# An FFN up-projection in three token blocks of 768 instead of two of 1152

## The chip, the core and the metric

The kernel runs on one NeuronCore of a Trainium2 chip. The metric is device time in microseconds (us) of one launch. Engines are named as the profile names them: PE (TensorE, matmuls) and PEld (its weight loads), DVE (VectorE), ACT (ScalarE), POOL (GpSimd), SP (SyncE, which here only issues DMAs).

## The reference

One encoder layer over 2048 + 256 tokens (2304 in all, two groups with the same weights), float32. The change lies in its second half, the convolutional FFN:

```
x = x + jnp.concatenate([m_out, a_out], axis=-1) @ w_out
h = rmsnorm(x, norm2_w)
u = centred_dwconv(h @ w_up, conv_w, conv_b)      # width 3 over tokens, 2*2816 columns
a, g = jnp.split(u, 2, axis=-1)
return x + (jax.nn.silu(g) * a) @ w_down          # then a last rmsnorm
```

D_MODEL is 1024, D_FF is 2816 = 22 column blocks of 128, so `w_up` has 44 column blocks, 22 for the gate g and 22 for a.

## The kernel before

Four stretches follow each other: a projection with preparation of q and k, mLSTM and attention interleaved, the output projection (`phase_c`), then the **up-pass** (`phase_u`) and the **down-pass** (`phase_e`). Tokens lie along the free dimension, channels on the 128 partitions.

**Products.** Every float32 operand is split in two float32r parts, hi (a rounded copy, made by ACT) and lo (the rest, a subtraction on DVE), and a product takes three matmuls: hi·hi, hi·lo, lo·hi. On top of that both passes use a 2x2 block scheme with seven products in place of eight (Strassen's, in Winograd's order), which needs sums of weight blocks and sums of token blocks.

**The up-pass.** The tokens are taken in blocks of `BLK`; `DT` holds the borders of the columns that a block computes (one or more columns beyond the block, for the width-3 convolution, which `carry` hands to the next block). For each block, 11 **groups** (`for gi, gr in enumerate(groups)`) each make two calls of `up`: one for two column blocks of the gate, one for the two of a. A call (`up_start` and its `rest`) loads two column blocks of `w_up` (`ru`, two DMAs of 512 KB on SP's queue), makes three sums `tw` and one in place on POOL, and runs seven products `mul` named "11", "21", "t2", "t1", "t3", "22", "t4". Each `mul` splits a 128x512 weight block into a `wu` (ACT copy, DVE subtraction; five rotating buffers, `WU`) and multiplies it with the operand of that name in `ops`, which holds a half of the block's tokens (n columns), hi and lo. The results come out of PSUM tiles p1, p2, p3 (`pa`, `pb`, `pc` in the profile) into `u` by ACT copies and DVE additions; p1 is accumulated on further after each copy. `conv` then makes `y` on ACT and two DVE multiply-adds per column block; in the last block ACT mends the two columns where the token groups meet. A group ends with two DVE products y·silu(g), four POOL sums for the down-pass's block scheme, and seven POOL-issued stores into DRAM `a_d`.

**Operands of the up-pass.** `n2_d` in DRAM holds the normed tokens; `n2_sums` makes their block sums on POOL (through DRAM `n2t_d`) and `n2_load` brings each of the seven operands in two halves (SP DMA, ACT copy, DVE subtraction). The sums for block b+1 are made in groups 3 to 6 (`SG`) of block b. The first three operands (`EARLY`) lie in the pool `d_1`, the others in `d_l` and `d_r`; all have one buffer, so those of block 1 are loaded when block 0 has done with them.

**The down-pass.** Seven products over 11 pairs of channel blocks and `G3` = 3 stretches of 384 token columns (z), with rings of weights (`dw` staged, `we` split) and of token operands (`te`, split in the same way). It is written behind the up-pass, in SBUF that the up-pass gives back.

**Order.** Each engine works through its own instructions in order. A list scheduler with a time model sorts the program's instructions into these queues at build time, so that products of the next call stand between those of the current one; `high_priority` pulls marked code ahead.

Of the kernel before, what the change touches and what calls it, by code (L numbers as in the profile page):

```python
# [35 lines left out]
BLK = 1152  # L36
# [10 lines left out]
NH = 580  # L47
NW = 2 * NH + 1
DT = (0, 2 * NH, T)
HB = BLK // 2  # L50
TW = T // 2
N2A, N2B = 1280, 1024
# [33 lines left out]
P0 = ((V, V),) * 4  # L86
P1 = ((V, V),) * 7
LOP = ()
DLAG = 6
SEGS = ((0, NT1), (NT1, NT))  # L90
# [944 lines left out]
def phase_c(g, sn, sp, pp, wps):  # L1035
# [64 lines left out]
    def tail_b(b, x, ps, r):  # L1100
        r = rstd_rows(g, ps, r, BT)
        for z in range(NCC):
            nc.vector.scalar_tensor_tensor(x[:, z], x[:, z], g.n2w[:, z:z + 1], r, ALU.mult, ALU.mult)
            if z % 4 == 3:
                if b * BT < N2A:
                    g.st.dma_start(g.n2_d[0][:, z - 3:z + 1, b * BT:(b + 1) * BT], x[:, z - 3:z + 1])
                if b * BT >= N2B:
                    g.st.dma_start(g.n2_d[1][:, z - 3:z + 1, b * BT - N2B:(b + 1) * BT - N2B], x[:, z - 3:z + 1])
        g.normed.add(b)
# [10 lines left out]
    for n, b in enumerate(order):  # L1120
        x, mx = nxt
        for z in range(4):
# [14 lines left out]
            if (n, z) > (5, 0) and sums:  # L1137

                n2_sums(g, sp, 0, sums.pop(0), tag="rn", bufs=2)
# [9 lines left out]
EARLY, LATE = OPS[:3], OPS[3:]  # L1149
# [7 lines left out]
def n2_load(g, ops, b, k, engs=("vector", "vector")):  # L1157
# [4 lines left out]
    if k[0] == "t":  # L1162
        i, h = SUMS[k]
        src = g.n2t_d[b, i, :, :, h]
    else:
        t = DT[b] - (0, N2B)[b] + n * (int(k[1]) - 1)
        src = g.n2_d[b][:, NCC // 2 * (int(k[0]) - 1):, t:t + n]
    for z in range(0, NCC // 2, 2):
# [3 lines left out]
        getattr(nc, engs[z // 2]).tensor_tensor(lo, f32(lo), f32(hi), ALU.subtract)  # L1172
# [6 lines left out]
def n2_sums(g, pool, b, c, engs=("gpsimd",) * 4, tag="tc", bufs=3):  # L1179
# [4 lines left out]
    m = n // 2  # L1184
    for z in range(2):
        rs = []
        for k in range(2):
            r = pool.tile([P, NH], F32, tag=tag, name=f"rn{b}_{c}_{z}_{k}", bufs=bufs)[:, 0:n]
            r = r.rearrange("p (h t) -> p h t", h=2)
            src = g.n2_d[b][:, c + NCC // 2 * k, DT[b] - (0, N2B)[b]:DT[b + 1] - (0, N2B)[b]].rearrange("p (h t) -> p h t", h=2)  # L1190
            nc.gpsimd.dma_start(r, src[:, :, z * m:z * m + m])
            rs.append(r)
        (b11, b12), (b21, b22) = ((r[:, 0], r[:, 1]) for r in rs)
        for eng, (o, p, q) in zip(engs, ((b11, b12, b11), (b12, b22, b12), (b22, b22, b11), (b21, b21, b22))):
            getattr(nc, eng).tensor_tensor(o, p, q, ALU.subtract)
        for k in range(2):
            nc.gpsimd.dma_start(g.n2t_d[b, k, :, c, :, z * m:z * m + m], rs[k])
# [17 lines left out]

def up_start(g, s1, bank, ops, b, jj, rs=None):
# [4 lines left out]
    m = n // 2  # L1221
# [6 lines left out]
    def mul(p, k, src, add=False):  # L1228
# [6 lines left out]
        for z in range(2):  # L1235
            for c in range(NCC // 2):
                for i, (aa, bb) in enumerate(((0, 0), (0, 1), (1, 0))):
                    nc.tensor.matmul(p[:, z], w[:, aa, c, :], ops[k][:, c, bb, z * m:z * m + m],  # L1238
                                     start=c == 0 and i == 0 and not add, stop=c == NCC // 2 - 1 and i == 2,
                                     skip_group_check=add)  # L1240
    p1, p2 = bank("a" + nm)[:, :, 0:m], bank("b" + nm)[:, :, 0:m]
# [8 lines left out]
    def rest(u1, u2):  # L1250


        u11, u12, u21, u22 = (u[:, k * n:k * n + n].rearrange("p (z t) -> p z t", z=2) for u in (u1, u2) for k in range(2))
# [10 lines left out]
        p3 = bank("c" + nm)[:, :, 0:m]  # L1264
# [14 lines left out]
def phase_u(g, tc, s1, pd, ops, first):  # L1279
# [5 lines left out]
    with ExitStack() as st:  # L1285
        sa = st.enter_context(tc.tile_pool(name="d_a", bufs=1, reuse_waits="tile"))
        for k in range(YB):
            sa.tile([P, BLK], F32, tag="y", name=f"place_y{k}", bufs=YB)
        for k in range(3):
            sa.tile([P, NH], F32, tag="tc", name=f"place_tc{k}", bufs=3)  # L1290
# [18 lines left out]
        late.update(n2_ops(sl2, 0, ("t3", "t1")))  # L1309
        late = {k: late[k] for k in LATE}  # L1310
        for k, e in zip(LATE, P0):
            n2_load(g, late, 0, k, engs=e)
# [3 lines left out]
        def bank(nm):  # L1316
            return banks(g, pd[(g.nbank + 1) // 2 % 2], "p" + nm)
        for b in range(ND):
            nn = DT[b + 1] - DT[b]
            if b:  # L1320
                ops = n2_ops(s1[0], b, EARLY)
                ops.update(n2_ops(sl, b, ("t4", "22")))
                ops.update(n2_ops(sl2, b, ("t3", "t1")))
                for k, e in zip(OPS, P1):
                    n2_load(g, ops, b, k, engs=e)
# [33 lines left out]
            for gi, gr in enumerate(groups):  # L1359
                if b < ND - 1 and SG <= gi < SG + NCC // 2:  # L1360
                    n2_sums(g, sa, b + 1, gi - SG)
                ygs = up(gr[0] + NFC)
# [6 lines left out]
                t1, t2, t4 = (sa.tile([P, NH], F32, tag="tc", name=f"tc{k}_{b}_{gi}", bufs=3)[:, 0:HB] for k in (1, 2, 4))  # L1369
# [11 lines left out]
def phase_e(g, tc, pd):  # L1381
# [5 lines left out]
    with ExitStack() as st:  # L1387
        sx = st.enter_context(tc.tile_pool(name="e_t", bufs=1, reuse_waits="tile"))
        for k in range(TR):
            sx.tile([P, 2, TG, CG], F32R, tag="t", name=f"place_t{k}", bufs=TR)  # L1390
        swa = st.enter_context(tc.tile_pool(name="e_w", bufs=1, reuse_waits="tile"))
        for k in range(WRA):
            swa.tile([P, 2, h], F32R, tag="w", name=f"place_wa{k}", bufs=WRA)
        sr = st.enter_context(tc.tile_pool(name="e_r", bufs=1, reuse_waits="tile"))
        for k in range(DW):
# [419 lines left out]
```

## Time and profile before

| | |
|---|---|
| three timed runs | 3369.89, 3371.27, 3371.71 us (median 3371.27) |
| the profiled execution | 3363.86 us, span 3361.9 us |
| granted PE clock, mean | 0.99 |
| busy, share of the span | PE 97%, PEld 90%, DVE 71%, ACT 54%, POOL 40% |
| up-pass alone on PE | about 1832.4 to 2836.6 us of the span |
| down-pass | from there to the end |

A row of a group of instructions gives line, engine, operation, tiles written and read, shapes and count, then busy time and mean duration, then the engine's idle time just before them and what ended it. A row of one line (in the view by source line) gives minimum / median / maximum duration in ns. A row of windows gives start:end, length, and for each engine its busy time and number of instructions, then granted clock, share of the DMA engines and GB/s. Busy time of DVE and POOL includes what an instruction waits after it has begun.

### The profile page before, as it was taken

How to read it: one execution, taken by the hardware profiler on the slowest of the kernel's cores; microseconds unless marked ns; L12 is line 12 of the kernel's file. 1: busy time of each engine (PE TensorE's matmuls, PEld its weight loads, DVE VectorE, ACT ScalarE, POOL GpSimd, SP SyncE). 2: the span in 40 equal slices, each digit the busy share in tenths (PEclk: the TensorE clock that was granted, in tenths of full speed). 3: DMA queues.
4: the chain of work that ended last, by engine and by line, in shares of the span. 5: the costliest groups of instructions: out<-in, count | busy, mean ns of one | idle time of the engine just before them, and what ended most of it. 6: DMA issues, size and time to landing. Idle time of an engine off the chain costs nothing. (4 is left out here: it accounts for less than half of the span.)

```text
span 3361.9 us, 57158 instructions
## 1 busy us (share of the span) xinstructions
PE 3262.6 (97%) x21366; PEld 3038.9 (90%) x21366; DVE 2399.9 (71%) x3721; ACT 1803.6 (54%) x3799; POOL 1355.2 (40%) x1710
## 2 busy tenths in 40 slices
PE   8899999999999999899999999999999999999998
PEld 6788888888888888788888999999999998999998
DVE  7866687777768778976765778978877776453573
ACT  5546666667666777655553544446555555323331
POOL 8653033213333323421245457744544442751112
PEclk9999999999999999999999999999999999999999
DMA  8665333343336444433347334424232223875563
GB/s 273 224 202 165 94 118 106 99 129 94 118 105 190 131 134 127 124 111 96 99 141 262 116 109 141 146 88 177 100 100 94 94 100 110 303 259 173 174 217 105
DMA packets 300636, 483.03 MB, mean 144 GB/s; under 512 B 36597, under 2 KB 186279, under 8 KB 300359
## 3 DMA queue, kind: packets, MB, share of 16 engines
q1 hardware_dynamic: 247543, 348.34, 32.7%
q0 software_dynamic: 36256, 121.60, 10.9%
q10 hardware_dynamic: 16560, 9.44, 0.9%
q8 instruction: 168, 2.75, 0.3%
q14 instruction: 109, 0.89, 0.1%
HBM read 337.37 MB, written 141.91 MB: 143 GB/s over the span
## 5 line engine op out<-in xcount | busy, mean ns | idle before, releaser
L634 DVE TENSOR_TENSOR pl<-ps,ph 128x512 fp32r<-128x512 f32 x520 | 353.9, 684 | 206.8 <-ACT ps L633 194.8
L1238 PE MATMUL pa<-nt,wut 128*128 128x290 f32 (+1 forms) x3168 | 447.0, 297 | 7.8 <-ACT u L1256 5.7
L632 ACT ACTIVATE ph<-ps 128x512 fp32r<-128x512 f32 x520 | 309.8, 596 | 248.7 <-PE ps L629 243.3
L1238 PEld LDWEIGHTS pa<-nt,wut 128*128 128x128 f32 x3168 | 431.1, 189 | 10.3 <-ACT u L1256 7.8
L603 DVE TENSOR_REDUCE mx<-px 128x1 f32<-128x512 f32 (+1 forms) x528 | 346.3, 673 | 94.3 <-PE px L602 92.2
L1348 DVE SCALAR_TENSOR_TENSOR y<-u,cw,y 128x1152 f32<-128x1152 f32 (+1 forms) x176 | 319.1, 1813 | 38.3 <-ACT yc L1346 17.3
L646 PE MATMUL pv<-ph,v 128*128 128x512 f32 (+1 forms) x1040 | 318.8, 401 | 0.8 <-ACT ph L632 0.3
L633 ACT ACTIVATE ps<-ps 128x512 f32<-128x512 f32 x520 | 310.2, 597 | 0.0
L1567 PE MATMUL et<-tet,wet 128*128 128x384 f32 x1584 | 279.0, 336 | 0.0
L1567 PEld LDWEIGHTS et<-tet,wet 128*128 128x128 f32 x1584 | 277.1, 188 | 0.0
L1081 PEld LDWEIGHTS po<-cmx,wo 128*128 128x128 f32 x1728 | 222.3, 192 | 9.7 <-DVE cmx L1069 1.5
L1081 PE MATMUL po<-cmx,wo 128*128 128x256 f32 x1728 | 226.4, 285 | 1.5 <-DVE cmx L1069 1.3
L1567 PE MATMUL e<-te,we 128*128 128x384 f32 x1188 | 213.5, 340 | 13.1 <-ACT te L1409 7.1
L1567 PEld LDWEIGHTS e<-te,we 128*128 128x128 f32 x1188 | 210.7, 190 | 14.5 <-ACT te L1409 7.3
L628 PE MATMUL ps<-qq,kk 128*128 128x512 f32 x520 | 214.9, 415 | 4.6 <-DVE mx L603 2.8
L602 PE MATMUL px<-kk,qq 128*128 128x512 f32 (+1 forms) x528 | 203.0, 412 | 4.1 <-DVE mx L603 2.4
L629 PE MATMUL ps<-qm,kl 65*128 65x512 f32 x520 | 205.9, 398 | 0.0
L792 PE MATMUL mj<-mn,wm 128*128 128x256 f32 x1296 | 197.9, 287 | 5.4 <-ACT og L808 3.4
L792 PEld LDWEIGHTS mj<-mn,wm 128*128 128x128 f32 x1296 | 182.7, 191 | 21.6 <-ACT og L808 3.8
L802 PEld LDWEIGHTS mv<-wm,mn 128*128 128x128 f32 x1296 | 183.1, 190 | 18.0 <-ACT qb L798 1.9
L802 PE MATMUL mv<-wm,mn 128*128 128x256 f32 x1296 | 196.9, 285 | 1.2 <-ACT qb L798 1.1
L646 PE MATMUL pv<-pl,v 128*128 128x512 f32 x520 | 191.6, 400 | 0.1
(310 smaller groups left out, 7244.9 us busy)
## 6 DMA issues: line engine op xcount, KB each, us to landing
mn<-n_d SPq DMA_DIRECT2D x216, 256.0 KB, 3.2
ru<-w_up SPq DMA_DIRECT2D x88, 512.0 KB, 3.6
a_d<-y POOLq DMA_DIRECT2D x88, 288.0 KB, 2.6
a_d<-tc POOLq DMA_DIRECT2D x66, 288.0 KB, 2.9
n_d<-n1T SPq DMA_DIRECT2D x18, 1024.0 KB, 5.3
dm<-nm_d POOLq DMA_DIRECT2D x72, 256.0 KB, 4.1
mjn<-n_d SPq DMA_DIRECT2D x72, 256.0 KB, 3.6
mvn<-n_d SPq DMA_DIRECT2D x72, 256.0 KB, 3.1
```

The lines of the kernel that those rows point to most:

```text
L603: nc.vector.tensor_reduce(s.mx[:, t, z0:z0 + 1], ps[:, 0:w], AX.X, ALU.max)
L628: nc.tensor.matmul(ps, kk[:, kc:kc + P], s.qq[:, 0:N], start=True, stop=False)
L632: nc.scalar.activation(ph, ps, AF.Exp)
L633: nc.scalar.activation(ps, ps, AF.Exp)
L634: nc.vector.tensor_tensor(pl, ps, f32(ph), ALU.subtract)
L646: nc.tensor.matmul(s.pv[0:HD if k in (1, 3) else P, 0:N], v, p, start=(kp == 0 and k == 0), stop=(2 * kp + 2 == s.nk and k == 5))
L792: nc.tensor.matmul(pj[:, o], s.w[c][:, a, o * P:(o + 1) * P], nT[c][:, :, h, :], start=(c + o + k == 0), stop=(c == NCC - 1 and k == 2 and ...
L802: nc.tensor.matmul(pv[:, o], nT[c][:, o, a, :], s.w[c][:, h, 256:512], start=(c + o + k == 0), stop=(c == NCC - 1 and k == 2 and o == 1))
L1081: nc.tensor.matmul(po[:, o], wo[z // 2][c][:, a, n], mx[c][:, h, :], start=(c == 0 and k == 0), stop=(c == NCC - 1 and k == 2))
L1238: nc.tensor.matmul(p[:, z], w[:, aa, c, :], ops[k][:, c, bb, z * m:z * m + m], start=c == 0 and i == 0 and not add, stop=c == NCC // 2 - 1 ...
L1348: nc.vector.scalar_tensor_tensor(y[:, s:e], u[:, s + k:e + k], cw[:, k, jj:jj + 1], y[:, s:e], ALU.mult, ALU.add)
L1567: nc.tensor.matmul(ps[m // 2][:, m % 2], w[:, aa, m * P:(m + 1) * P], t[:, bb], start=p == 0 and n == 0, stop=p == NP - 1 and n == 2)
```

## The change

`BLK` goes from 1152 to 768, so the up-pass has three blocks, whose computed columns are 772, 768 and 764; a half has 386, 384 and 382 columns. A `mul` is now 12 matmuls of that width into one PSUM bank instead of 24 of 290 or 286 into two; `bank1` rotates through eight single banks (before: four pairs). The three DVE/POOL choices `P0`, `P1`, `engs` were all "vector" in use and are gone. `n2_sums` takes a whole half at once (four sums and four DMAs per channel pair, before twice that for smaller pieces) with a buffer tag `rn` of its own. Four operands are now EARLY, and have a second set of buffers in a new pool `d_b`: groups 7 to 10 of block b load those of block b+1, one operand a group. The other three (LATE) still wait for the block's end. The pools of the down-pass are put in another order: its `dw` and first `we` ring lie over `d_1`'s first operands, its `te` ring over `d_b`, which the third block does not use, and its first loads are marked high priority.

```diff
-BLK = 1152
+BLK = 768
-NH = 580
+NH = 386
-DT = (0, 2 * NH, T)
+DT = (0, 2 * NH, 4 * NH - 4, T)
-N2A, N2B = 1280, 1024
+N2R = ((0, 1024), (768, 1792), (1536, T))
-EARLY, LATE = OPS[:3], OPS[3:]
+EARLY, LATE = OPS[:4], OPS[4:]
...
-    m = n // 2
-    for z in range(2):
-        rs = []
-        for k in range(2):
-            r = pool.tile([P, NH], F32, tag=tag, name=f"rn{b}_{c}_{z}_{k}", bufs=bufs)[:, 0:n]
...
+    rs = []
+    for k in range(2):
+        r = pool.tile([P, 2, NH], F32, tag="rn", name=f"rn{b}_{c}_{k}", bufs=2)[:, :, 0:n]
+        t = DT[b] - N2R[b][0]
+        nc.gpsimd.dma_start(r, g.n2_d[b][:, c + NCC // 2 * k, t:t + 2 * n].rearrange("p (h t) -> p h t", h=2))
...
+def bank1(g, pools, name):
+    k = g.nbank = g.nbank + 1
+    return pools[k // 4 % 2].tile([P, 512], F32, tag=f"q{k % 4}", name=name, bufs=1)
...
-        for z in range(2):
-            for c in range(NCC // 2):
-                for i, (aa, bb) in enumerate(((0, 0), (0, 1), (1, 0))):
-                    nc.tensor.matmul(p[:, z], w[:, aa, c, :], ops[k][:, c, bb, z * m:z * m + m],
...
+        for c in range(NCC // 2):
+            for i, (aa, bb) in enumerate(((0, 0), (0, 1), (1, 0))):
+                nc.tensor.matmul(p, w[:, aa, c, :], ops[k][:, c, bb, 0:n],
...
+        sb = st.enter_context(tc.tile_pool(name="d_b", bufs=1, reuse_waits="tile"))
+        n2_ops(sb, "place", EARLY)
...
-                ops = n2_ops(s1[0], b, EARLY)
+                ops = nxt
                 ops.update(n2_ops(sl, b, ("t4", "22")))
-                ops.update(n2_ops(sl2, b, ("t3", "t1")))
-                for k, e in zip(OPS, P1):
-                    n2_load(g, ops, b, k, engs=e)
+                ops.update(n2_ops(sl2, b, ("t3",)))
+                for k in LATE:
+                    n2_load(g, ops, b, k)
...
+                if b < ND - 1 and gi == SG + NCC // 2:
+                    nxt = n2_ops(s1[0] if b % 2 else sb, b + 1, EARLY)
+                if b < ND - 1 and 0 <= gi - SG - NCC // 2 < len(EARLY):
+                    n2_load(g, nxt, b + 1, EARLY[gi - SG - NCC // 2])
...
-        fetch_w(WA)
-        fetch_t(2)
+        with tc.high_priority(offset=MPRI):
+            fetch_t(1)
+            fetch_w(WA)
+            fetch_t(1)
```

How the instructions stand, at three places. In the names, `pa`, `pb`, `pc` are p1, p2, p3; after the name of a product comes the block's number, then the first column block of the call; the last number is a buffer.

PE, one call in the last block, before:

```order
L1238 MATMUL pb1_38_32237<-n21_1_28357,wu21_1_38_32265 128x286 x24
L1238 MATMUL pa1_38_32236<-nt2_1_28358,wut2_1_38_32300 128x286 x24
L1238 MATMUL pc1_38_32328<-nt1_1_28362,wut1_1_38_32329 128x286 x19
L1238 MATMUL pa1_38_32236<-nt3_1_28361,wut3_1_38_32357 128x286 x24
L1238 MATMUL pa1_16_32468<-n11_1_28356,wu11_1_16_32470 128x286 x2
L1238 MATMUL pc1_38_32328<-n22_1_28360,wu22_1_38_32385 128x286 x24
```

and after:

```order
L1237 MATMUL pc2_10_31617<-nt1_2_28618,wut1_2_10_31618 128x382 x12
L1237 MATMUL pa2_10_31561<-nt2_2_28617,wut2_2_10_31601 128x382 x12
L1237 MATMUL pb2_34_31724<-n21_2_28616,wu21_2_34_31740 128x382 x12
L1237 MATMUL pa2_10_31561<-nt3_2_29837,wut3_2_10_31634 128x382 x12
L1237 MATMUL pa2_34_31723<-n11_2_28615,wu11_2_34_31725 128x382 x12
L1237 MATMUL pc2_10_31617<-n22_2_29836,wu22_2_10_31650 128x382 x12
```

A product has half as many matmuls, each a third wider, and products of the next call still stand between two that use the same PSUM tile.

DVE, about one call of the last block, before:

```order
L1234 TENSOR_TENSOR wu22_1_40_32863<-tw4_1_40_32713,wu22_1_40_32863 128x512
L1259 TENSOR_TENSOR u1_40_32774<-pb1_40_32715,u1_40_32774 128x572
L1348 SCALAR_TENSOR_TENSOR y1_17_32683<-u1_17_32529,cw_23218,y1_17_32683 128x1152
L1234 TENSOR_TENSOR wut4_1_40_32891<-ru1_41_32708,wut4_1_40_32891 128x512
L1348 SCALAR_TENSOR_TENSOR y1_17_32683<-u1_17_32529,cw_23218,y1_17_32683 128x1151
L1234 TENSOR_TENSOR wu11_1_18_32948<-ru1_18_32939,wu11_1_18_32948 128x512
L1367 TENSOR_TENSOR y1_17_32683<-y1_17_32683,y1_39_32451 128x1152
```

and after:

```order
L1234 TENSOR_TENSOR wu22_2_16_32580<-tw4_2_16_32490,wu22_2_16_32580 128x512
L1234 TENSOR_TENSOR wu21_2_40_32670<-ru2_40_32646,wu21_2_40_32670 128x512
L1351 SCALAR_TENSOR_TENSOR y2_38_32465<-u2_38_32379,cw_23173,y2_38_32465 128x768
L1351 SCALAR_TENSOR_TENSOR y2_38_32465<-u2_38_32379,cw_23173,y2_38_32465 128x767
L1234 TENSOR_TENSOR wu11_2_40_32655<-ru2_40_32646,wu11_2_40_32655 128x512
L1234 TENSOR_TENSOR wut2_2_40_32693<-tw2_2_40_32651,wut2_2_40_32693 128x512
L1258 TENSOR_TENSOR u2_17_32528<-pa2_16_32491,u2_17_32528 128x382
```

The kinds and their number per call are the same and the token-wide ones are a third shorter, but the weight subtractions (128x512) keep their size, and a third block makes all of them once more.

SP's queue at the change from the second block to the third, which is new:

```order
L1201 DMA ru2_1_30005<-w_up 128x1024
L1463 DMA te11_0_0_33329<-a_d0_67 128x4x384
L1463 DMA te11_0_1_33343<-a_d4_68 128x4x384
L1463 DMA te11_0_2_33354<-a_d8_69 128x3x384
L1463 DMA te11_1_0_33439<-a_d0_67 128x4x384
L1201 DMA ru2_24_30166<-w_up 128x1024
L1168 DMA nt3_2_29837<-n2t_d_64 128x2x382 x2
L1168 DMA n22_2_29836<-n2_d2_63 128x2x382 x2
L1168 DMA nt4_2_29835<-n2t_d_64 128x2x382 x2
```

and the same loads of `te` before, at the end of the up-pass:

```order
L1206 DMA ru1_20_33417<-w_up 128x1024
L1206 DMA ru1_21_33418<-w_up 128x1024
L1443 DMA dw11_0_33717<-w_down 128x512
L1443 DMA dw11_1_33722<-w_down 128x512
L1452 DMA te11_0_0_33726<-a_d0_66 128x4x384
L1452 DMA te11_0_1_33730<-a_d4_67 128x4x384
```

The first four `te` loads have moved from behind the up-pass's last weights to the start of the third block, ahead of that block's LATE operands.

More of the change, by code (lines that the diff above doesn't have):

```diff
@@ L1136, in phase_c @@
             post(b, z, x, po, acc)
-            if (n, z) > (5, 0) and sums:
-                n2_sums(g, sp, 0, sums.pop(0), tag="rn", bufs=2)
+            if (n, z) > (4, 0) and sums:
+                n2_sums(g, sp, 0, sums.pop(0))
         prev = (b, x, acc)
@@ L1220, in up_start @@
     n = (DT[b + 1] - DT[b]) // 2
-    m = n // 2
     nm = f"{b}_{jj}"
@@ L1308, in phase_u @@
         sl2 = st.enter_context(tc.tile_pool(name="d_r", bufs=1, reuse_waits="tile"))
[L1309 to L1312, printed above, removed]
+        late.update(n2_ops(sl2, 0, ("t3",)))
+        for k in LATE:
+            n2_load(g, late, 0, k)
         ops.update(late)
@@ L1714, in body @@
                 f()
-            first = [up_start(g, s1, lambda nm: banks(g, pd[(g.nbank + 1) // 2 % 2], "p" + nm), ops, 0, NFC, rs)]
+            first = [up_start(g, s1, lambda nm: bank1(g, pu, "p" + nm), ops, 0, NFC, rs)]
             g.c_end()
             s_wo.close()
-            pd.append(pool(s5, "d_v", bufs=1, space=PSUM))
-            phase_u(g, tc, s1, pd, ops, first)
+            pu.append(pool(s6, "d_v", bufs=1, space=PSUM))
+            phase_u(g, tc, s1, pu, ops, first)
+        s6.close()
+        pd = [pool(s5, f"d_e{k}", bufs=1, space=PSUM) for k in range(2)]
+        g.nbank = 2
         phase_e(g, tc, pd)
```

82 lines of the change are left out of this document (43 added, 39 removed).

## Prediction

> **What bounds the kernel now.** I read the page's first part, then cut the span at the up-pass, at whole groups inside it, at the change of block and at the first 53 us of the down-pass. Each row: window, length, busy time and count of PE, PEld, DVE, ACT and POOL, granted clock, share of the DMA engines, GB/s.
>
> ```profile
> PE 3262.6 (97%) x21366; PEld 3038.9 (90%) x21366; DVE 2399.9 (71%) x3721; ACT 1803.6 (54%) x3799; POOL 1355.2 (40%) x1710
> ...
> 1832.40:2836.60 1004.20, 991.98 (x7388) 987.80 (x7386) 777.11 (x683) 513.90 (x850) 525.50 (x471) 1.00 0.34 115
> 2055.00:2188.80 133.80, 133.75 (x993) 133.34 (x992) 120.36 (x90) 60.67 (x94) 104.27 (x100) 1.00 0.43 140
> 2322.60:2411.80 89.20, 85.55 (x636) 84.39 (x635) 81.77 (x72) 54.60 (x88) 40.26 (x31) 1.00 0.50 172
> 2500.90:2768.50 267.60, 267.60 (x2022) 267.60 (x2021) 193.50 (x181) 144.66 (x265) 124.32 (x116) 1.00 0.28 95
> 2836.60:2890.00 53.40, 40.36 (x207) 39.24 (x208) 31.80 (x26) 20.02 (x27) 33.16 (x43) 0.84 0.74 254
> ```
>
> The up-pass is PE's: in the six quiet groups (2500.9:2768.5, 44.6 us each) PE is busy throughout and DVE 72%. In the three groups in which POOL makes the next block's token sums (2055:2188.8) DVE is at 90% and PE still loses nothing. At the change of block DVE is at 92% and PE loses 3.7 us. The first stretch of the down-pass loses most.
>
> What a matmul costs at each width: counts per 100 us where PE is full at 290 and at 286 columns, and one unbroken piece of the chain of waits at 384.
>
> ```profile
> 1900.00:2000.00 100.00, 100.00 (x746) 100.00 (x745) 1.00 0.30 104
> 2600.00:2700.00 100.00, 100.00 (x757) 100.00 (x756) 1.00 0.28 95
> 2992.65 178.69 PE et L1567 x1020
> ```
>
> That is 134.0, 132.1 and 175.2 ns. The last two lie on a line of 0.44 ns a column plus 6.3 ns a matmul.
>
> **Why POOL matters to DVE.** By source line: min/median/max ns in the quiet stretch 2500:2800 (first, third row) and in 2000:2200 with the sums (second, fourth, fifth), then over the run.
>
> ```profile
> L1234 DVE TENSOR_TENSOR wut<-tw,wut x27: 684/694/1342, 2500.5 to 2789.8; 128x512 fp32r<-128x512 f32 x27
> ...
> L1234 DVE TENSOR_TENSOR wut<-tw,wut x16: 677/1376/3708, 2016.8 to 2181.2; 128x512 fp32r<-128x512 f32 x16
> ...
> L1348 DVE SCALAR_TENSOR_TENSOR y<-u,cw,y x55: 1404/1419/3857, 2502.2 to 2799.8; 128x1152 f32<-128x1152 f32 x28, 128x1151 f32<-128x1151 f32 x27
> ...
> L1348 DVE SCALAR_TENSOR_TENSOR y<-u,cw,y x36: 1404/1822/4362, 1999.3 to 2191.7; 128x1151 f32<-128x1151 f32 x18, 128x1152 f32<-128x1152 f32 x18
> ...
> L1259 DVE TENSOR_TENSOR u<-pb,u x9: 749/751/757, 2008.6 to 2193.6; 128x580 f32<-128x580 f32 x9
> ...
> L1367 DVE TENSOR_TENSOR y<-y,y x44: 1343/1358/2455, 1889.9 to 2855.0; 128x1152 f32<-128x1152 f32 x44
> ...
> L1245 POOL TENSOR_TENSOR tw<-ru x44: 1277/1294/2403, 1787.9 to 2787.2; 128x512 f32<-128x512 f32 x44
> L1371 POOL TENSOR_TENSOR tc<-y x22: 1416/1440/2259, 1892.2 to 2841.7; 128x576 f32<-128x576 f32 x22
> L1195 POOL TENSOR_TENSOR rn<-rn x32: 682/704/1890, 1668.9 to 2167.9; 128x290 f32<-128x290 f32 x16, 128x286 f32<-128x286 f32 x16
> ```
>
> The same subtraction takes 0.69 or 1.38 us. Only DVE instructions that read two SBUF tiles stretch: the additions that read PSUM (L1259) stay at 0.75. POOL's sums stretch too, up to twice. The timeline shows how:
>
> ```profile
> 2184.86 3.77 DVE L1348 SCALAR_TENSOR_TENSOR y<-u,cw,y 128x1151 f32<-128x1151 f32 x2
> 2185.08 2.33 POOL L1246 TENSOR_TENSOR tw<-tw,ru 128x512 f32<-128x512 f32 x1 [0.21 <-issue]
> 2187.37 2.42 POOL L1247 TENSOR_TENSOR ru<-ru,ru 128x512 f32<-128x512 f32 x1
> 2188.56 1.78 DVE L1234 TENSOR_TENSOR wut<-ru,wut 128x512 fp32r<-128x512 f32 x1
> ```
>
> The last subtraction starts at 2188.56, ends at 2190.34 and needs 0.68, so it ran from 2189.66: POOL's sum ended at 2189.79. The two engines take turns, with some 0.13 us of overlap at each hand-over. So DVE and POOL share something, and what counts is the sum of their unhindered work.
>
> **That sum, before.** A group has 14 weight subtractions (0.685), 8 convolution steps (1.404), 2 products (1.358) and 6 additions (0.75) on DVE: 28.0 us; on POOL 8 weight sums (1.29) and 4 of `y` (1.44): 16.1. Together 44.1 us of work in a group of 44.6. In 2055:2188.8 stand three groups (90 DVE instructions, 84.0 us) and on POOL 24 + 12 + 22 sums (31.0 + 17.3 + 15.4): 147.7 us of work in 133.8, a rate of 1.10 with PE full and DVE 90% busy. If DVE's last 10% could be filled in proportion, the most is 1.10 / 0.90 = 1.23.
>
> **The change, part by part.**
>
> Matmuls. 7392 (44 calls x 7 x 24) at 133.05 ns, 983.5 us, become 5544 (66 x 84) of 384 columns on average at 175.2, 971.3 us: −12 us of PE, if PE still sets the pace, 29.4 us a group. The Trainium skill (TensorE: Matmul & The Clock Gate, Back-to-back issue gap) gives N/2.4 + 2.5 ns, which makes the saving 1848 x 2.5 ns = 4.6 us; the rows show 175.2 at 384 columns where that rule has 162.5, so the rows decide.
>
> DVE and POOL, per group of 768 tokens. From 512 columns in 0.685 to 1152 in 1.358 DVE takes 1.05 ns a column: steps of 768 take 1.00, products 0.95, additions of 384 0.55. POOL's sums of 384, between 0.70 at 286 and 1.29 at 512, take 0.95. DVE: 9.6 + 8.0 + 1.9 + 3.3 = 22.8; POOL: 10.3 + 3.8 = 14.1. Together 36.9 us against PE's 29.4: PE's pace would need a rate of 1.25 where 44.1 / 44.6 = 0.99 was enough. The cause is the weight side: 22 more calls bring 154 subtractions (105 us) and 88 weight sums (113 us), and only the token side shrinks with the block.
>
> The rest of that work. Token sums: 2 blocks x 16 sums of 0.95, 30 us (before 32 x 0.70 = 22). Operand halves: 28 DVE subtractions of some 0.96, 27 us (before 14 of 1.36, 19 us); 16 of them lie in groups 7 to 10, 12 at the changes of block. Four `te` halves now fall into the third block: 6.6 us by the DVE row of the next part. The up-pass's work is 33 x 36.9 + 30 + 27 + 7 = 1282 us.
>
> The time from it. At 1.10 the up-pass takes 1165 us, at 1.23 1042. I take 1.19, nearer to the upper end since a DVE that lags is never idle for want of work, and below it since in 2055:2188.8 POOL still found DVE idle one tenth of the time: 1077 us. With some 6 us for the start, which waits as before, 1083 against 1004: **+79 us** (+44 to +167).
>
> Hidden (rows below): ACT's 154 more copies, 0.62 us each, 96 us, bring its 514 us to some 620 of 1083. DMA: 44 more loads of 512 KB add 23 MB to the 115 GB/s of the up-pass, 0.34 of the engines. POOL's own queue: 33 groups of 14.1 us of sums and 7 stores of 0.56 us, and the token sums, are some 630 us, waits aside. PSUM: eight single banks give a call more room than four pairs; worth 0 to −4 us, taken as 0, since PE's idle time before L1238 is small:
>
> ```profile
> L1233 ACT ACTIVATE wut<-ru 128x512 fp32r<-128x512 f32 x28 | 17.5, 625 | 5.4 <-PE pb L1238 5.4
> ...
> L1357 POOL DMA_DIRECT2D a_d<-y x84 | 47.0, 559 | 80.2 <-DVE y L1367 80.2
> ...
> L1238 PE MATMUL pa<-nt,wut 128*128 128x290 f32 (+1 forms) x3168 | 447.0, 297 | 7.8 <-ACT u L1256 5.7 <-ACT nt L1171 2.0
> ```
>
> Second buffers and change of block. Before, the one change cost 3.7 us. Now there are two, each with three operands left to fetch and 6 DVE halves, in the sum already. At the second, four `te` loads of 768 KB stand ahead of the LATE loads on SP's queue, and their halves ahead of theirs on ACT and DVE; whoever waits there is PE, at "t3". I take no more than the work already counted (0 to +10).
>
> Down-pass start. PE, DVE and ACT there:
>
> ```profile
> 2843.63 1.01 PE L1567 MATMUL e<-te,we 128*128 128x384 f32 x2 [7.10 <-ACT te L1409]
> 2845.43 21.94 PE L1567 MATMUL e<-te,we 128*128 128x384 f32 x114 [0.79 <-DVE te L1410]
> 2872.59 12.63 PE L1567 MATMUL e<-te,we 128*128 128x384 f32 x62 [5.22 <-DVE we L1410]
> ...
> 2843.61 1.76 DVE L1410 TENSOR_TENSOR te<-te 128x1536 fp32r<-128x1536 f32 x1 [2.19 <-ACT te L1409]
> ```
>
> In 53.4 us it does 207 matmuls, 36.3 us of work: 17 lost. With `te` in place the first matmul still waits for the last calls' convolution steps that stand ahead of the first two `we` subtractions on DVE: 0.55 + 0.96 (ACT) + 2.0 + 0.7 = 4.2 us after the second last product, 2.1 of them covered. With as much again for the next weights, 5 us stay: **−12 us** (0 to −17).
>
> Sum: +79 − 12 = +67 on the profiled 3363.9 us, **3430 us**. That execution is 7.4 us below the median of the runs, 3371.3; I leave 3430, inside that difference.
>
> **Rivals.**
> - *The shared work still hides* (faster). If turns between the engines cost DVE nothing that PE notices, as in 2055:2188.8, PE keeps 29.4 us a group: 971 + 17 for start and changes, 988, −16, and −12 at the down-pass: **3336 us**. It decides from a rate of 1.25 on, over all 33 groups. For it: PE lost nothing at 1.10. Against: 1.10 already took 90% of DVE.
> - *Only the laden groups are bound.* At exactly 1.25 quiet groups run at PE's pace; the eight with token sums (40.7 us of work) take 32.5, the eight with operands (38.8) 31.0: 33 x 29.4 + 25 + 13 + 11 (changes) + 6 + 6 = 1031, +27 − 12: **3379 us**.
> - *No overlap at all.* DVE steps with two SBUF inputs and POOL's sums exclude each other for their whole length, additions alone running beside them: (1282 − 33 x 3.3) + 6 = 1179, +175 − 12: **3527 us**. Against it stands the 0.13 us of overlap above; for it, that DVE's additions and waits do not all find POOL at work. The Trainium skill (SBUF — State Buffer, Who interferes with whom) says this: the loser "fully blocks" for the whole instruction. By that rule the time is this rival's; the trace agrees with the turns and with who is hit, and not with the last tenth of a microsecond.
> - *Second buffers that do not help*: LATE operands or `te` loads hold PE up at each change by the 5 to 10 us they need to land; it adds to any of the others and decides none.
>
> **How the numbers follow.** The forecast has 0.60, the shared work hidden 0.15, laden groups only 0.13, no overlap 0.12. A measurement tells 0.2% (6.7 us) from no change. The first rival is faster; the second is slower unless the down-pass gains its full 17 us and the changes cost nothing: faster 0.16, same 0.05, slower 0.79. The forecast's own range is 3395 to 3515. For 8 in 10 I go down to 3345, which takes in the laden groups and leaves most of the first rival out, and up to 3515, where most of "no overlap" is left out.
>
> **What would show it.** Right: DVE over 93% busy through the up-pass, weight subtractions near 1.2 us or more on average, PE idle before L1237 put down to DVE and ACT, groups of 30 to 34 us, longest where the token sums stand; matmuls at 175 ns; a gap of some 5 us before the first `e`. Wrong: PE full in quiet groups at 29.4 us (a rate of 1.25 is reached), or POOL's weight sums so late that PE waits for them while DVE idles, or long waits for `nt` at the changes.

## The result and the profile after

The changed kernel takes 3540.86 us (median of four runs, 3536.42 to 3544.26) against 3370.58 for the kernel before on the same chip: the ratio is 1.051, 95% interval 1.0489 to 1.0531. The forecast had the sign and, at 3430 us (range to 3515), less than half of the size.

The page of the changed kernel, its line of busy times:

```profile
PE 3315.2 (94%) x19518; PEld 3062.6 (87%) x19518; DVE 2680.7 (76%) x4065; ACT 1916.4 (54%) x4209; POOL 1546.4 (44%) x1887
```

Windows of it, in the same columns as before: the up-pass; four groups of block 0 with token sums; ten groups of block 1; nine of block 2; the down-pass's first 53.4 us.

```profile
1833.50:3027.00 1193.50, 1049.97 (x5518) 1015.31 (x5517) 1055.09 (x1020) 624.24 (x1248) 732.41 (x676) 0.94 0.34 117
1958.80:2128.30 169.50, 138.48 (x679) 134.24 (x678) 146.13 (x122) 69.81 (x129) 107.99 (x105) 0.87 0.35 117
2277.60:2600.40 322.80, 297.80 (x1617) 289.92 (x1616) 297.96 (x294) 173.03 (x351) 198.79 (x187) 0.97 0.30 107
2652.60:2980.90 328.30, 283.93 (x1509) 270.36 (x1508) 276.25 (x271) 179.88 (x397) 187.39 (x172) 0.96 0.27 96
3027.00:3080.40 53.40, 51.46 (x287) 51.46 (x288) 30.98 (x25) 21.20 (x33) 30.46 (x36) 0.97 0.73 247
```

The up-pass grew from 1004.2 to 1193.5 us (+189; forecast +79), the down-pass (to the span's end) fell from 525.3 to 507.5 (−18; forecast −12). PE now idles 143.5 us of the up-pass, and its matmuls took 190 ns each instead of 175, at a granted clock of 0.94 (175.2 / 0.94 would be 186). A group takes 42.4 us among the token sums, 32.3 in block 1, 36.5 in block 2, which differs from block 1 mainly by the mending; PE alone would need 29.4. DVE is busy for 86%, 92% and 84% of these: it is not the full engine that the prediction expected.

The change of block is another matter. In the code the EARLY operands of the next block are loaded in groups 7 to 10; in the queues they stand elsewhere, as the width of their halves tells (768 columns in block 1, 764 in block 2). The eight halves of block 1 stand at 1858.7 to 1968.3 us, among the token sums. The eight of block 2 stand at the first change, beside block 1's six LATE ones, by source line (the subtractions of the halves):

```profile
L1170 DVE TENSOR_TENSOR nt<-nt x8: 942/949/2067, 2248.0 to 2265.9; 128x764 fp32r<-128x764 f32 x4, 128x768 fp32r<-128x768 f32 x4
L1170 DVE TENSOR_TENSOR n<-n x6: 940/943/950, 2238.7 to 2263.0; 128x764 fp32r<-128x764 f32 x4, 128x768 fp32r<-128x768 f32 x2
```

There, by windows, DVE is busy throughout:

```profile
2227.40:2276.60 49.20, 43.43 (x223) 42.64 (x222) 49.17 (x50) 31.63 (x58) 32.05 (x22) 0.90 0.59 194
```

What DVE's instructions cost in block 1 (minimum, median, maximum in ns, by source line):

```profile
L1234 DVE TENSOR_TENSOR wut<-ru,wut x23: 679/1086/3089, 2349.0 to 2528.0; 128x512 fp32r<-128x512 f32 x23
...
L1351 DVE SCALAR_TENSOR_TENSOR y<-u,cw,y x46: 1003/1808/3292, 2342.0 to 2525.1; 128x768 f32<-128x768 f32 x46
```

The unhindered sizes are as forecast (0.68 and 1.00 us); the median convolution step takes 1.8 times its size. Who waits for whom among the token sums (engine, line waited for; us, times, longest):

```profile
ACT y L1371 <- DVE y L1351: 38.4, 8, 8.1
POOL tw L1244 <- DVE wut L1234: 37.1, 6, 11.0
...
PE pa L1237 <- ACT u L1255: 22.7, 6, 6.5
```

So most of PE's waiting in this stretch is not for DVE but for ACT's copies out of PSUM. These stand in ACT's queue behind the silu (L1371), which waits up to 8.1 us for a convolution step that POOL's sums have stretched. Over the whole up-pass it is about half; the largest rows of PE's waits there:

```profile
PE pa L1237 <- ACT u L1255: 55.6, 29, 6.5
PE pc L1237 <- DVE wut L1234: 31.9, 15, 3.7
PE pa L1237 <- DVE wu L1234: 27.4, 15, 4.2
PE pc L1237 <- ACT u L1255: 9.7, 8, 3.3
```

All rows together, PE waits 65 us for ACT's copies and 74 us for DVE's subtractions and additions, and in blocks 1 and 2 DVE's part is the larger one.

### The profile page after: what moved, and what is told of

Read it like the earlier page. It is cut to its first block, busy times and chain, and to the rows that moved or that the text cites. A ratio compares the mean times of both kernels' runs of the same rounds, so it can differ in the third digit from the quotient of the medians.

```text
span 3534.5 us, 54951 instructions
## 1 busy us (share of the span) xinstructions
PE 3315.2 (94%) x19518; PEld 3062.6 (87%) x19518; DVE 2680.7 (76%) x4065; ACT 1916.4 (54%) x4209; POOL 1546.4 (44%) x1887
## 5 line engine op out<-in xcount | busy, mean ns | idle before, releaser
L1237 PE MATMUL pa<-nt,wut 128*128 128x386 f32 (+2 forms) x2376 | 483.9, 356 | 66.4 <-ACT u L1255 55.6
L1237 PEld LDWEIGHTS pa<-nt,wut 128*128 128x128 f32 x2376 | 446.5, 201 | 80.6 <-ACT u L1255 67.5
L1351 DVE SCALAR_TENSOR_TENSOR y<-u,cw,y 128x768 f32<-128x768 f32 (+1 forms) x264 | 416.9, 1579 | 11.2 <-ACT y L1344 7.3
L1237 PE MATMUL pa<-n,wu 128*128 128x386 f32 (+2 forms) x792 | 172.7, 355 | 28.6 <-DVE wu L1234 27.4
```

The costliest lines, as they stand in the source:

```text
L1237: nc.tensor.matmul(p, w[:, aa, c, :], ops[k][:, c, bb, 0:n], start=c == 0 and i == 0 and not add, stop=c == NCC // 2 - 1 and i == 2, skip_ ...
L1351: nc.vector.scalar_tensor_tensor(y[:, s:e], u[:, s + k:e + k], cw[:, k, jj:jj + 1], y[:, s:e], ALU.mult, ALU.add)
```

## The experiments

Single runs have one execution; four of the changed kernel spread over 8 us, so differences under 10 us are not read from one. The runs come from several chips, on which the kernel before took 3365.2 to 3375.3 us (3370.6 beside the changed kernel); differences between runs hold that too.

**1. POOL's weight sums: left out, moved to DVE, and doubled in the kernel before.**

```diff
 # e1, changed kernel: no sums; "t2", "t1", "t3", "22" take unsummed blocks
-    nc.gpsimd.tensor_tensor(t1, a21, a22, ALU.add)      # and the three others
+    t1, t2, t4 = a21, a11, a12
 # e2, changed kernel: the four sums on DVE
-    nc.gpsimd.tensor_tensor(t1, a21, a22, ALU.add)      # and the three others
+    nc.vector.tensor_tensor(t1, a21, a22, ALU.add)
 # e4, kernel before: POOL's instructions for the sums 4 -> 8 a call
+    nc.gpsimd.tensor_tensor(t1, a21, a22, ALU.add)      # repeated, as are t2 and, twice more, t4
```

> The changed kernel without POOL's four weight sums per call: the products t1, t2 and 22 read unsummed weight blocks, everything else is as it was. Theory S (DVE steps with two SBUF inputs and POOL's sums take turns, and the up-pass lasts as long as their work together needs): the work of a group falls from 36.9 to 26.6 us, below PE's 29.4, so groups of some 30 us, up-pass 1000 us against 1193, the whole about 3345 us. Theory Q (in-order queues: PE's copies out of PSUM stand on ACT behind instructions that wait for DVE's convolution steps, and a product of 2.1 us is too short to cover that): groups stay above 33 us, up-pass above 1110, the whole above 3450. Theory P (single banks or the PE clock after short stalls): no change, 3535.

> The changed kernel with the four weight sums of a call made by DVE instead of POOL (0.69 instead of 1.29 us each). Theory S: DVE has 28.3 us a group, POOL 3.8, together 32.1 instead of 36.9; with the rate of 1.08 that the changed kernel reached the up-pass takes about 1046 us instead of 1193, the whole about 3390 us. A theory in which DVE's own instructions are the bound (22.8 us a group, now 28.3): slower, above 3560 us. Theory Q: about the same, 3500 to 3560.

> The kernel before with four of POOL's weight sums of each call made twice over (same results), so 5.2 us more of POOL work a call. Theory S: the work of a group rises from 44.1 to 54.4 us; at a rate of 1.08 a group takes 50 us instead of 44.6 and the whole about 3500 us. If POOL's work hides behind PE in two blocks: 3370 us, within 15 us.

Measured: 3357.8, 3413.3 and 3498.8 us; the kernel before 3365.2. The up-pass without sums, by windows:

```profile
1833.00:2850.00 1017.00, 984.18 (x5509) 972.57 (x5508) 835.51 (x1019) 623.66 (x1247) 326.19 (x414) 0.99 0.40 138
```

and with the sums on DVE:

```profile
1833.00:2905.00 1072.00, 1009.84 (x5531) 986.14 (x5531) 1007.51 (x1282) 629.04 (x1252) 329.04 (x417) 0.98 0.38 131
```

Without the sums PE is busy 97% and the clock 0.99: 183 us of the changed kernel's time hang on instructions that hold POOL, an engine 44% busy, and the third block's own matmuls and loads cost next to nothing. Without the sums no product waits for one either; but with the sums on DVE, where products still do, 128 of the 183 us are gone. On DVE the same sums cost 56 us; DVE is then 94% busy and PE still 94%. Doubled, they slow the old blocks by 134 us. All three agree with one shared resource, and the queues by themselves (above 3450 us without sums) are not the cause; none says yet how much of both engines' work it lets through.

**2. The two engines by themselves.** Nothing of the computation is left: stretches of DVE and POOL instructions on fixed tiles, in the up-pass's shapes, without waits between them.

```diff
+        both([lambda: sub(512)] * 100, [])                            # alone
+        both([], [lambda: pool(512)] * 52)
+        both([lambda: sub(512)] * 100, [lambda: pool(512)] * 52)      # together
+        both([step] * 70, [lambda: pool(512)] * 52)
+        both([add] * 120, [lambda: pool(512)] * 52)                   # add reads PSUM
+        both(mix * 4, gmix * 2 * 4)                                   # four groups of the up-pass
```

> The disputed rate by itself; nothing of the computation is left, the output is zeros. Stretches in order: 100 DVE subtractions of 128x512 alone; 52 POOL sums of 128x512 alone; both at once; 70 DVE convolution steps of 768 beside 52 POOL sums; 120 DVE additions that read PSUM beside 52 POOL sums; the instruction mix of four groups of the up-pass on both engines without any waits between them. Turns theory: alone 0.69 and 1.29 us; subtractions and sums together run at 1.00 to 1.15 of their unhindered work (135 to 117 us for 68 + 67), the additions unhindered (67 us for both), and the mix of four groups (91 us on DVE, 78 of it with two SBUF inputs, 56 on POOL) in 120 to 134 us. The rate of 1.19 that the prediction took would give the mix 124 us; free running 91.

The six stretches in that order (start:end, length, busy time and count of DVE and POOL, clock, DMA); the third to fifth end with POOL's last sum:

```profile
10.35:82.98 72.63, 69.25 (x100) 0.00 (x0) 1.00 0.00 0
83.73:153.33 69.60, 1.20 (x1) 65.62 (x52) 1.00 0.00 0
154.01:240.48 86.47, 84.59 (x53) 82.46 (x52) 1.00 0.00 0
276.67:375.94 99.27, 97.39 (x52) 95.27 (x52) 1.00 0.00 0
397.54:467.39 69.85, 65.92 (x118) 65.84 (x52) 1.00 0.00 0
470.96:594.23 123.27, 120.71 (x122) 75.60 (x48) 1.00 0.00 0
```

Alone a subtraction takes 0.69 and a sum 1.26 us. Together 52 of each (101.6 us of work) took 86.5 us: a rate of 1.17. With 51 convolution steps (1.00 each, from the row above) it is 116.8 in 99.3: 1.18. Each pair passes the turn twice and overlaps by some 0.15 us at each. The additions that read PSUM lengthen nothing. The mix of four groups, 147.6 us by the prediction's own sum, took 123.3, though POOL was through after 79 and DVE went on alone: a rate of 1.20, 30.8 us a group. So the number 1.19 was right for two engines that never wait for anybody else. In the kernel block 1 came to 36.9 / 32.3 = 1.14, block 2 to 1.01, and the whole up-pass to 1282 / 1187 = 1.08.

**3. The mending of two columns in the last block.**

```diff
 # e3: the mending left out
-                if cut < BLK:
+                if False:
 # e7: same result, with the steps cut at the border instead
+                    steps = [(0, 0, cut), (0, cut + 1, BLK), (2, 0, cut - 1), (2, cut, BLK - 1)]
```

> The changed kernel without ACT's mending of the two columns at the border of the token groups in the last block (six small ACT instructions per call, two of which wait for DVE's convolution steps). Theory Q: the groups of the third block, 36.2 us though they have neither token sums nor operand loads, fall to the 32 us of the second block, the whole by 40 us to about 3495. Theory S: less than 10 us, since no shared work is taken away: 3525 to 3540.

> The changed kernel, in which the last block's convolution steps are cut at the border between the two sequences (four DVE steps in place of two, leaving out the column that must not be added) and the ACT instructions that save and mend the two border columns are gone. Same result, 22 x 2 more DVE instructions of about 0.06 us fixed cost. Queue theory (ACT's mend waits for the DVE step, PSUM copies stand behind it on ACT, PE behind those): as without the mending, 3502 us, plus 1 to 5: about 3505. Rival, the gain without mending came from less ACT work or a changed schedule: 3525 to 3540.

Measured: 3502.4 and 3516.3 us, 38 and 25 us under the changed kernel (the second has 88 more DVE steps, not 44, and by their shortest durations a cut step takes 0.735 + 0.467 us in place of 1.003: 88 x 0.2 = 17 us of DVE work, where 1 to 5 us were expected). With the cut, block 2 runs at 33.4 us a group instead of 36.5. What the mending did there shows in the waits of the changed kernel, 2652.6:2980.9:

```profile
ACT y L1355 <- DVE y L1351: 87.8, 31, 5.1
```

and in a stretch of its timeline (start, duration):

```profile
2872.99 4.71 DVE L1351 SCALAR_TENSOR_TENSOR y<-u,cw,y 128x768 f32<-128x768 f32 x2
...
2873.55 1.02 POOL L1383 TENSOR_TENSOR tc<-y,tc 128x384 f32<-128x384 f32 x1
2874.53 1.29 POOL L1247 TENSOR_TENSOR tw<-ru,tw 128x512 f32<-128x512 f32 x1
...
2877.80 0.67 ACT L1355 ACTIVATE y<-u,yc,cw 128x1 f32<-128x1 f32 x2 [5.11 <-DVE y L1351]
...
2878.36 2.03 PE L1237 MATMUL pb<-n,wu 128*128 128x382 f32 x10 [0.76 <-DVE wu L1234]
```

Two steps that need 2.0 us take 4.7: DVE loses to two POOL sums in a row. ACT, whose next instruction is the mend of two columns, stands still for 5.1 us, with everything behind it. PE, which still had products to do, loses 0.76 us of that here.

**4. The token sums, all of which the scheduler had put in block 0.** (Without them the operands of blocks 1 and 2 are those of block 0.)

```diff
-                    n2_sums(g, sa, b + 1, gi - SG)
+                    pass
```

> The changed kernel without the token sums of blocks 1 and 2 (32 POOL sums of 0.95 us, their 8 x 4 DMAs; all of them stand in block 0). By work alone, 30 us at the rate of 1.08: 3540 - 28 = 3512 us. If they cost block 0 what its groups were longer than those of block 1 (41 against 32 us in five groups, and some in two more): 3540 - 50 = 3490, with block 0's groups at 32 us. If block 0 is slow for another reason (lower clock, operands): 3540.

Measured: 3487.2 us, −54: the second case. (Between the two traced executions it is 49, all of it in block 0, whose last product ends at 2226.9 us in place of 2276.6.) The same stretch of block 0, by DVE's products (L1374, two a group: busy time and count, then clock and DMA), in the changed kernel:

```profile
1958.80:2128.30 169.50, 9.55 (x8) 0.87 0.35 117
```

and without the token sums:

```profile
1958.80:2128.30 169.50, 9.50 (x10) 0.97 0.31 109
```

Five groups stand where four stood, and 30 us of POOL work had cost about 50.

**5. Shorter turns, and more buffers for the sums.** Each POOL sum in two or four instructions (the latter with the cut of experiment 3), and six buffers in place of three (in the kernel without token sums, which has the space).

```diff
 # e11 (n = 2), e12 (n = 4)
+        for k in range(n):
+            nc.gpsimd.tensor_tensor(*(t[:, k * m:k * m + m] for t in (o, p, q)), op)
 # e15
-    tag="tmp", ..., bufs=3
+    tag="tmp", ..., bufs=6
```

> The changed kernel, with every POOL weight sum (512 columns) and y sum (384) cut into two instructions of half the width; the same work in 24 turns a group instead of 12. If turns overlap by 0.13 us at each hand-over, 12 more of them give 1.6 us a group, 33 x 1.6 = 51: about 3490 us. If what hurts is the length of the turn that a DVE step loses (1.29 us, or two in a row), more than that: 3420 to 3480. If only the total work counts: 3540. If the shorter turns let DVE go first so often that POOL's sums come too late for PE: above 3540.

> The same with four instructions for each sum (128 and 96 columns, some 0.33 and 0.25 us), and with the convolution steps cut at the border in place of the mending (3516 us by itself). Turn length: 3380 to 3440. Hand-overs only: 36 x 0.13 = 4.7 us a group at most, down to PE's pace: 3400 to 3450. Total work: 3516. POOL late: above 3516.

> The kernel without the token sums (3487 us; it frees the space), with six buffers for POOL's weight sums in place of three, so that POOL need not wait until DVE has read those of the call before. If POOL's late start is what keeps the pair from its rate, the quiet groups fall from 32 us toward 33.6 less 24 hand-overs of 0.15, 30 us: 3487 - 33 x 2.3 = about 3412 us. If not, 3480 to 3490, with the wait of POOL's sums for DVE's subtractions gone or small.

Measured: 3518.8, 3549.2 and 3504.5 us, that is −22 against the changed kernel, +33 against the cut alone, +17 against no token sums. None came near its gain; the halves gained something, the quarters lost. By source line (minimum, median, maximum in ns), sums of 512 columns in the changed kernel,

```profile
L1245 POOL TENSOR_TENSOR tw<-tw,ru x12: 1282/1462/2025, 2348.3 to 2524.2; 128x512 f32<-128x512 f32 x12
```

of 256 in the one with halves,

```profile
L1247 POOL TENSOR_TENSOR tw<-tw,ru x128: 712/914/2242, 1854.6 to 2979.5; 128x256 f32<-128x256 f32 x128
```

and of 128 in the one with quarters:

```profile
L1247 POOL TENSOR_TENSOR tw<-tw,ru x252: 444/472/1972, 1866.5 to 3017.4; 128x128 f32<-128x128 f32 x126
```

The minima lie on 0.16 us plus 2.2 ns a column: a cut sum costs one more 0.16, about what the hand-over gives back. In quarters POOL is the full engine. Block 1 of it, by windows:

```profile
2340.00:2530.00 190.00, 169.44 (x902) 162.41 (x902) 151.60 (x161) 93.89 (x194) 187.36 (x302) 0.96 0.28 99
```

With six buffers the waits of POOL's first sum, in the view of waits, are mostly no longer for DVE but for the weights:

```profile
POOL tw L1244 <- DMA ru<-w_up: 200.2, 40, 16.1
```

Its groups alternate around the same mean of 32 us. But POOL's start still hangs on DVE: the weight loads that it now waits for wait in their turn, on SP's queue, for DVE's subtractions of the weights before (344 us of waits between 2236 and 2600 us). So whether POOL's late start matters stays open.

**6. Second buffers, the ring, the order of the first fetches.**

```diff
 # e16: all seven operands at the change of block, one set of buffers
-                ops = nxt
+                ops = n2_ops(s1[0], b, EARLY)
 # e14: the down-pass's pools in the order of before
+        sx, swa, sr first; EGAP gone
 # e17, kernel before: only the fetch order of the change
-        fetch_t(2)                      # after fetch_w(WA)
+            fetch_t(1); fetch_w(WA); fetch_t(1)      # high priority
```

> The changed kernel without the second buffers: all seven operands of blocks 1 and 2 are loaded at the change of block into the buffers of the block before. If the second buffers hide what they were made for, each change gets longer by the halves and loads of four more operands (16 DVE and ACT steps of about 1 us and their DMAs), less what groups 7 to 10 lose to them now: 3540 + 2 x (3 to 15) = 3546 to 3570 us. If the DVE work only moves: 3540.

> The changed kernel with the down-pass's rings where they lay before, not over the second buffers. If the second buffers are what let the te operands in early: the 18 us that the down-pass gained come back, 3558 us, with PE waiting before the first e matmuls as before. If the te loads in the last change of block cost as much as they bring: 3540.

> The kernel before, with the one line of the change that stands in the down-pass's start: the first te operand is fetched ahead of the first two weights, and these fetches go ahead of the last group's work. If the order of the fetches is what gained the down-pass its other 12 us: 3366 - (6 to 12) = 3354 to 3360 us. If the loads stay bound to when the old operands' space comes free: 3366, the same.

Measured: without second buffers 3524.0 us, 17 less than with them (13, if each is taken against the kernel before on its chip): where the up-pass is short of DVE and POOL, fetching early only moves their work. It had moved eight halves in among the token sums and eight more to the first change, so that the changes are hardly longer without it (54 and 52 us for 49 and 52). With the old ring 3546.1, too near to tell from the whole time, but the traces tell: PE's idle time behind the last up-pass matmul, summed over the down-pass from the trace's records, is 17.1 us before, 5.1 after, 11.4 with the old ring, 11.8 in the kernel before with the new fetch order. The first e matmuls by the timeline, in the changed kernel,

```profile
3028.94 51.23 PE L1580 MATMUL e<-te,we 128*128 128x384 f32 x284 [1.96 <-ACT we L1420]
```

with the old ring,

```profile
3030.94 1.01 PE L1579 MATMUL e<-te,we 128*128 128x384 f32 x2 [5.09 <-ACT we L1419]
```

and in the kernel before with the new order:

```profile
2846.05 1.01 PE L1569 MATMUL e<-te,we 128*128 128x384 f32 x2 [4.84 <-ACT we L1409]
```

Ring and order each bring some 6 us there. By itself the order brings nothing: 3365.46 against 3365.49 us, ratio 0.9996 (0.9986 to 1.0005), since in the traced executions its up-pass ends 5 us later.

**7. Versions.** The sums made once, in block 0, stored in DRAM and loaded by blocks 1 and 2; the same with the cut and with block 0's sums on DVE; and the kernel before with the fetch order and the cut.

```diff
 # e6, e8
+        for t, k in ((t2, 1), (t1, 0), (a21, 2), (t4, 3)):
+            g.nc.sync.dma_start(t, g.ws_d[k][jj // 2])       # blocks 1 and 2
+                nc.gpsimd.dma_start(g.ws_d[k][jj // 2], t)   # block 0
 # e18: e17 with the cut steps of e7
```

> The changed kernel, in which block 0 stores POOL's four weight sums of every call in DRAM and blocks 1 and 2 load them (256 KB each) in place of making them. Turns theory (DVE steps that read two SBUF tiles and POOL's sums exclude each other, and their sum per group, 33.6 us against PE's 29.4, sets the pace): blocks 1 and 2 shrink as they did without the sums, from 375 and 386 us to 334 and 333, block 0 stays: 3540 - 41 - 53 = about 3446 us, with the group periods of blocks 1 and 2 at 27 to 32 us. Rival, transfers (0.75 MB more a call, on SP's queue, into the three sum buffers): the loads come late and PE waits for them, 3480 or more. Rival, the third block's matmuls and weight loads as such: 3535 again.

> The two together, and the weight sums of block 0 made on DVE: block 0 as with sums on DVE (330 us against 315 without sums), blocks 1 and 2 as without sums, no mending. Turns and queue theory: 3357 + 15 - (0 to 10) = 3362 to 3372 us, the same as before the change within 0.2%. Rival, late transfers: over 3400. If the second buffers of the down-pass (-18 us) and the shorter matmul time (-12) come out whole while nothing else is lost: 3340.

> The same, and the convolution steps of the last block cut at the border in place of the mending. PE is full in the quiet groups of the kernel before, so the mending can cost it only at the down-pass's start, where the last calls' steps stand ahead of the first operands on ACT and DVE: 0 to 4 us less than without the cut, 3350 to 3360.

Measured: 3472.9 us for the first. Blocks 1 and 2 took 333 and 334 us, as expected; block 0 was 30 us longer than in the changed kernel, with 88 more stores in POOL's queue. The second: 3369.0 us, ratio 1.0005 (0.9994 to 1.0016), no different from before, as forecast. A stretch of block 1 of the first, by windows:

```profile
2400.00:2500.00 100.00, 99.95 (x569) 99.62 (x568) 79.17 (x100) 59.90 (x123) 24.89 (x33) 1.00 0.53 168
```

and the up-pass of the second:

```profile
1833.00:2857.00 1024.00, 993.64 (x5538) 978.83 (x5537) 905.28 (x1193) 602.40 (x1130) 379.99 (x501) 0.99 0.57 193
```

In the first, PE is full at last, at 175.7 ns a matmul, as forecast. In the second, the changes of block (39 and 45 us where a group takes 29.4) and block 0 use up the 12 us of the shorter matmuls and the 18 of the down-pass. The third: 3361.98 us, just above the 3350 to 3360 expected, ratio 0.9993 (0.998 to 1.0006). No version beat the kernel before by more than a run can tell.

## Why the prediction was right or wrong

- *Matmuls, −12 us*: right. 175.7 ns at 386 to 382 columns wherever PE is full (experiment 7). In the changed kernel itself the lower granted clock took this back and more (190 ns on average).
- *Work per group, 36.9 us*: right in its parts (0.68, 1.00, 1.28 us minima), and the mix by itself ran at 1.20 of its sum. The 30 us of token sums were counted rightly too, but placed in two blocks; they all stood in block 0. The operand halves stood elsewhere too: not 16 in groups 7 to 10 and 12 at the changes, but 8 among the token sums, 14 at the first change and 6 at the second.
- *The rate of 1.19*: the step that failed, with its lower bound of 1.10. The bounds were read from a stretch in which PE set the pace, so what PE loses when the two engines set it did not show there. As a property of the two engines by themselves 1.19 was right (1.17 to 1.20, experiment 2), in part by luck, since it was picked between two bounds and no row gave it. As the rate of the whole up-pass it was not: 1.08, below the lower bound. The 110 us that were missing (1193 for 1083) can be put down by estimate: the 31 groups outside the changes at 32.3 instead of 31.0 us, 31 x 1.3 = 40; token sums at some 50 instead of 25; the mending, 25 to 38 where nothing was forecast. That is 90 to 103. The two changes of block, 49 and 52 us, are long by the work that stood in them; counted from the trace at each kind's shortest duration, the two engines did 57.0 us of work in 49.2 and 58.5 in 52.2 there, rates of 1.16 and 1.12, against 161.0 in 169.5 (0.95) among the token sums and 330.8 in 328.3 (1.01) in block 2.
- *ACT hidden*: wrong, and it is about half of the mechanism behind that (65 us of PE's waits). ACT is 52% busy in the up-pass, as forecast (624 us for 620), but its queue holds instructions that wait for a DVE step (silu, mending) ahead of PSUM copies that PE waits for. A DVE step that loses two turns can then cost PE several us. Shown for the mending by experiment 3; for the silu it is read from the waits, and was not tried by itself. The other half (74 us) are waits for DVE's own subtractions and additions, though DVE was idle 12% of the time. Without POOL's weight sums (experiment 1) the two kinds of waits fall to 12 and 19 us, so both hang on the turns.
- *POOL's queue hidden*: wrong among the token sums, about 50 us for 30 of work; whether its queue or its turns did it was not separated. *DMA* and *PSUM hidden*: nothing in the waits speaks against it; the PSUM banks were not tried alone.
- *Second buffers*: that they do not help was one of the rivals, and it held; without them one execution was 13 to 17 us shorter.
- *Down-pass, −12*: it was −18, outside the 0 to −17 forecast. PE's idle time fell by 12.0 us, 17.1 to 5.1; another 6 came from shorter matmuls, half of that in the first 53 us (179 ns each for 195), where the clock was 0.97 in place of 0.84.
- *Rivals*: "no overlap at all" gave 3527 us and came nearest, by a wrong way: there are 0.15 us of overlap at each hand-over, and the rest is waiting around the ring. The Trainium skill (SBUF — State Buffer, Summary: rules for kernel authors) says that when DVE has two SBUF inputs and the POOL instruction reads SBUF, the second one to issue "fully blocks" until the first finishes. The trace agrees with who is hit (additions that read PSUM stayed at 0.56 us); by the rule 52 subtractions and 52 sums would take 101.6 us, and they took 86.5.
- *What would show it*: the longest groups among the token sums came (42 us, beyond the 30 to 34 named), and PE waiting for ACT and DVE; DVE over 93% busy did not (88% over the up-pass), and that was the sign that waits, not work, had the last word. Nor did weight subtractions of 1.2 us on average (1.06), or matmuls at 175 ns.

## What to carry to other kernels

Two engines that take turns can be summed, but the sum, divided by the rate that they reach alone (1.17 to 1.20 here), is only a floor for the time: expect more wherever a third engine's queue holds their results ahead of work that the bound engine needs. A block size that repeats a per-block cost (here weight splits and sums) should be priced on the engine that pays it, even at 40% busy. A conditional detail that is free while PE is full, like the mending of two columns, may cost 25 us once it is not.

## What the hardware showed unexpectedly

POOL's elementwise sums and DVE's two-input steps overlap by about 0.15 us at each hand-over, which is also about POOL's fixed cost for an instruction (0.16 us), so cutting instructions shorter gained little (22 us with halves, in one run) or lost (33 us with quarters). A DVE step can lose to two POOL sums in a row (4.71 us for two steps that need 2.0). And a PE wait can cost more than its own length. In the clock records of the up-pass each of 29 falls is to half the clock, for 3.4 or 6.8 us, and begins during a wait of 1.9 to 6.5 us or at most 1.5 us after it, though not every wait of that length is followed by one (3.73 us at 2885.0 us is not). The stretch after the longest wait, by the window and by the timeline, where twelve matmuls take 3.86 us and twelve others soon after 2.29:

```profile
2009.60:2016.40 6.80, 3.25 (x10) 3.25 (x11) 4.23 (x5) 2.64 (x5) 1.83 (x3) 0.50 0.37 131
...
2013.15 3.86 PE L1237 MATMUL pa<-nt,wut 128*128 128x386 f32 x12 [6.53 <-ACT u L1255]
2018.77 2.29 PE L1237 MATMUL pc<-n,wu 128*128 128x386 f32 x12
```

Over the token sums that makes the granted clock 0.87. What the lower clock added to the whole time was not tried by itself.
